# One transformer block on one Trainium2 core: values ahead of transposes in the rounds of neighbourhood attention

## The chip, the cores and the metric

The kernel runs on one core of one Trainium2 chip. A time is device time in microseconds (us) of one execution; the kernel before took 1009.01 us (median of three runs, 1008.9 to 1009.04). Engines are named as the profile names them: PE multiplies matrices (PEld is its weight loads, which overlap its matmuls), DVE and ACT are the vector and scalar engines, POOL is GpSimd, SP issues DMAs.

## The reference

One layer with 1024 latent tokens (16 rows of 64 columns, width 1024) and 256 context tokens. Only the attention matters here; the pooling mixer beside it, the projections and the MLP are the rest of the time.

```python
def row_block(r):                      # one of 16 grid rows; 8 heads of 64
    rs = clip(r - kh // 2, 0, rows - kh)               # a window of 8 rows
    s_loc = einsum('bnqhd,brnkhd->bhnqrk', q_r, k_b) * scale
    s_loc = where(col_mask, s_loc + bias, -inf)        # 16 columns, learned 2-D bias
    s_ctx = einsum('bnqhd,bkhd->bhnqk', q_r, k_ctx) * scale
    p = softmax(concatenate([s_loc, s_ctx], axis=-1))
    o = einsum('bhnqrk,brnkhd->bnqhd', p_loc, v_b) + einsum('bhnqk,bkhd->bnqhd', p_ctx, v_ctx)

mix_x = concatenate([pool_mixer(u_x), attn_x], axis=-1) @ w_out
x = x + gt1 * rmsnorm(mix_x, g_post_mix)
x = x + gt2 * rmsnorm(sq_relu_mlp(modulate(rmsnorm(x))))
```

## The kernel before

The kernel is one program with stages in a row: input norm and projections, attention (212 to 323 us of the span), output projection, MLP. In the attention stage the 16x64 grid is cut into eight tiles of 16 rows by 8 columns (128 tokens). A unit is one pair of heads j (0 to 3) with one tile m (0 to 7); there are N = 32 units, and round i of one loop works on several units at once, at different steps:

- `scores(i)` (L1259, PE): queries times keys for both heads, 12 matmuls of high and low parts, into the two PSUM tiles S (one per head e; there are only these two). An inner tile (m 1 to 6) has 640 keys: three local tiles and the context. An end tile (m 0 and 7) has 512.
- `biased(i, e)` (L1279, DVE): adds the table of biases to S, writes sp to SBUF and its smallest value nm. For e = 0 it also calls `share(i - 1)`: the reciprocal of the sums (L1294, DVE), spread out by POOL as rb (L1296).
- `exps(i, e)` (L1290, ACT): the exponential of sp, in place, with its sums.
- `turn(i)` (L1312, PE): transposes. First rb and, for an inner tile, the fifth key block of each head, into the side columns of pa (256 to 447) and of pz (0 to 191); then four key blocks of both heads into the two PSUM tiles T.
- `fifth_kept(i)` (L1326, ACT): copies the side columns of pa and of pz to px in SBUF.
- `turn_kept(i, 0)` on ACT and `turn_kept(i, 1)` on DVE (L1331): copy the two T tiles to the page pt in SBUF.
- `values(i)` (L1346, PE): the weights pt and px times the values, 8 or 10 matmuls (the profile shows 16 or 20), into columns 0 to 127 of pa, or 128 to 255 for odd i.
- `weighed(i)` (L1356, DVE): those columns of pa times the transposed rb, into the page f.

pa and pz are one PSUM tile of 512 columns each, with one buffer. Each engine runs its instructions in the order in which the code issues them (`in_order` around the loop), and waits between engines are put in by the framework from what instructions read and write. The order of the calls in the loop is therefore the order of the work. Other work of the stage is issued in the rounds, mostly on POOL and SP: bias tables (`built`), key and query parts, sums and loads for later stages. Behind the loop stand the last two units' steps, mixed with the first sums of the output projection (`first_sums`).

Of the kernel before, what the change touches and what calls it, by code (L numbers as in the profile page):

```python
# [108 lines left out]
def hybrid_block(ctx, tc, x, ctx_in, w_mod, mod_pages, w_u, b_mod, gp1, gp2, w_in, pool_w, rpb, w_out, w1, w2, vectors,  # L109
                 mask, edge, out):  # L110
    nc = tc.nc
# [1118 lines left out]
    with (  # L1230
# [12 lines left out]
        def scores(i):  # L1243
            j, m = units[i]
            inner = 0 < m < NM - 1
            n = NKEY if inner else 4 * P
            o = 1 if m == 0 else 0
            q = qparts[j, m // 4]
            ck = [a[:, j * CTX : (j + 1) * CTX] for a in kcs]
            cols = slice((m % 4) * P, (m % 4 + 1) * P)  # L1250
            heads = [slice(e * HD, (e + 1) * HD) for e in range(2)]
            S = [ps_s.tile([P, 1024], F32, tag="S", name=f"S{j}_{m}_{e}") for e in range(2)]
            ts = slice((m - 1) * P, (m + 2) * P) if inner else slice((m + o - 1) * P, (m + o + 1) * P)
            local = [a[:, ts] for a in kparts[j]]
            parts = ((128, local), (512, ck)) if inner else ((0, ck), (256, local))
            for c0, k in parts:
                for n_q, n_k in ((0, 0), (0, 1), (1, 0)):
                    for e, hs in enumerate(heads):
                        nc.tensor.matmul(S[e][:, c0 : c0 + k[0].shape[1]], q[n_q][hs, cols], k[n_k][hs],  # L1259
                                         start=(n_q + n_k == 0), stop=(n_q == 1))  # L1260
            scored[i] = S

        def biased(i, e):
            j, m = units[i]
            inner = 0 < m < NM - 1
            n, o, S = NKEY if inner else 4 * P, 1 if m == 0 else 0, scored[i]
            halves = lambda a: a.rearrange("p (a b) -> p a b", a=2)
            t = tabs[j % 2][e]
            sp = att.tile([P, NKEY], F32, tag="sp", name=f"sp{j}_{m}_{e}", bufs=6)[:, :n]
            if inner:  # L1270
                s, bt, to = S[e][:, 128:768], t[:, :NKEY], sp
            else:
                s, to = halves(S[e][:, 0:512]), halves(sp)
                if o:
                    bt = halves(t[:, 2 * P : 8 * P])[:, :, P:]
                else:
                    bt = halves(t[:, NLOC : NLOC + 512])
            nm = sm(f"nm_{i}_{e}", 1, 6)
            nc.vector.tensor_tensor_reduce(out=to, in0=s, in1=bt, scale=1.0, scalar=BIG, op0=add, op1=ALU.min,  # L1279
                                           accum_out=nm)  # L1280
            probs[i, e] = sp
            least[i, e] = nm
            if e == 0 and i > 0:
                share(i - 1)

        def exps(i, e):
            if e == 0:
                sums[i] = sm(f"su_{i}", 2, 4)
            sp = probs[i, e]
            nc.scalar.activation(sp, sp, AF.Exp, bias=least[i, e], scale=-1.0, accum_out=sums[i][:, e : e + 1])  # L1290
# [11 lines left out]
        def turn(i, t=None, more=None):  # L1302
            inner = 0 < units[i][1] < NM - 1
            if t is None:
                t = [bank(f"T{i}_{h}") for h in range(2)]
            sides = both_sides[i] = more or both_sides[None]
            turned[i] = t
            halves = [slice(h * HD, (h + 1) * HD) for h in range(2)]

            def both(to, src):  # L1310
                for h, hs in enumerate(halves):
                    nc.tensor.transpose(to(h), src(hs), ident[hs, hs])  # L1312

            both(lambda h: sides[h][:, :HD], lambda hs: shares[i][hs])
            for e in range(2 if inner else 0):
                both(lambda h: sides[h][:, (e + 1) * HD : (e + 2) * HD], lambda hs: probs[i, e][hs, 4 * P : 5 * P])
            for c in range(4):
                for e in range(2):
                    o = (4 * e + c) * HD
                    both(lambda h: t[h][:, o : o + HD], lambda hs: probs[i, e][hs, c * P : (c + 1) * P])  # L1320

        def fifth_kept(i):
            n = (3 if 0 < units[i][1] < NM - 1 else 1) * HD
            fifths[i] = att.tile([P, 384], F32, tag="px", name=f"px{i}", bufs=4).rearrange("p (h t) -> p h t", h=2)
            for h in range(2):
                nc.scalar.copy(fifths[i][:, h, :n], both_sides[i][h][:, :n])  # L1326

        def turn_kept(i, h, copy):
            if h == 0:
                turns[i] = page(f"pt{i}").rearrange("p (e i t) -> p e i t", e=2, i=4)  # L1330
            copy(turns[i].rearrange("p e i t -> p (e i) t")[:, :, h * HD : (h + 1) * HD],  # L1331
                 turned[i][h].rearrange("p (a t) -> p a t", a=8))
# [18 lines left out]
        def weighed(i):  # L1351
            j, m = units[i]
            if m == 0:
                heads[j] = page(f"f{j}")
            to = heads[j].rearrange("p (m h t) -> p m h t", h=2, t=HD)[:, m, ::-1, ::-1]
            nc.vector.tensor_tensor(to, pa[:, (i % 2) * P : (i % 2 + 1) * P].rearrange("p (h t) -> p h t", h=2),  # L1356
                                    fifths[i][:, :, :HD], mul)

        N = len(units)
# [88 lines left out]
        with in_order(ET.PE, ET.Activation, ET.DVE, ET.SP) as projected:  # L1448
# [34 lines left out]
            for i in range(N):  # L1483
                if i in LOADS:
                    weight_load(0, kks[LOADS.index(i)])
                if i == N - 2:
                    G1 = gate_page("a")
                if i > 3:
                    weighed(i - 4)
                if i == 0:  # L1490
                    gain = mod_gain(gp1, att.tile([P, 256], F32, tag="gp", name="gpa"), nc.sync)
                    accs["sh"] = page("accsh2")
                    nc.sync.dma_start(accs["sh"], kept_row)
                if i == 2:
                    mod_gate("a", accs["a"], gain, rest_of_bank)
                if i in (5, 6):
                    for k in (2 * i - 10, 2 * i - 9):
                        nc.sync.dma_start(sa2[k], s3[k])
                low()
                scores(i)  # L1500
                biased(i, 0)
                if i < N - 1:
                    biased(i, 1)
                if 8 < i and i % 8 == 3:
                    right_added(i // 8 - 1)
                if 8 < i and i % 8 == 7:
                    add_to(heads[i // 8 - 1][:, :512], sa2[i // 8 - 1])
                for f, *args in jobs.get(i, ()):
                    f(*args)
                if block_copies and (i < 4 or 6 < i):  # L1510
                    block_copied()
                for _ in range(SUMS.count(i)):
                    block_summed()
                if i == 2:
                    late_query = part_page("qP0_1", False)
                    qparts[0, 1] = late_query[:, :512], late_query[:, 512:]
                    high_part(qT[0][1], qparts[0, 1][0])
                if i > 1:
                    turn(i - 2)
                    fifth_kept(i - 2)  # L1520
                if i == 2:
                    turn_kept(0, 0, nc.scalar.copy)
                    column_sums("sc", accs["sc"], lambda name: pa[:, :256])
                if i == N - 1:
                    turn_kept(i - 2, 0, nc.scalar.copy)
                    turn_kept(i - 2, 1, nc.vector.tensor_copy)
                    biased(i, 1)
                exps(i, 0)
                if i == 2:
                    column_sums("sh", accs["sh"], rest_of_bank)  # L1530
                if 2 < i < N - 1:
                    turn_kept(i - 2, 0, nc.scalar.copy)
                exps(i, 1)
                if i == 0:
                    key_parts(2, 0, True, "lo")
                    key_parts(2, 1, True, "lo")
                    query_parts(2, 0, False, "lo")
                if 1 < i < N - 1:
                    turn_kept(i - 2, 1, nc.vector.tensor_copy)
                if i == 2:  # L1540
                    low_part(qT[0][1], *qparts[0, 1])
                for filler in fillers.get(i, ()):
                    last_query(*filler)
                if i > 2:
                    values(i - 3)
            values(N - 3)

            x, s1 = [], halves_of("so1_")

# [989 lines left out]
```

## Time and profile before

| | us |
|---|---|
| median of the runs | 1009.01 |
| profiled execution | 1009.41 |
| its span, first to last instruction | 1007.6 |
| attention: first scores to the start of the last values | 212.6 to 322.4 |
| PE busy / DVE / ACT / POOL, whole span | 997.7 / 799.9 / 580.9 / 208.8 |
| mean granted clock of PE | 0.999 |

A line of the timeline gives the start in us from the span's start, the time in us, the engine, the source line, the operation, output<-inputs, and in brackets the idle time of that engine ahead of it with what ended it. Matmul ends are modelled, so PE reads as nearly always busy; its weight loads (PEld) show when its queue moved. A line of the chain gives start, time, engine, output and source line.

### The profile page before, as it was taken

To read this page: it belongs to the slowest core of one execution; us is meant where nothing else is said; L and a number is where in the kernel's file an instruction comes from. 1 tells how busy PE (TensorE), PEld (TensorE's weight loads), DVE (VectorE), ACT (ScalarE), POOL (GpSimd) and SP (SyncE) were. 2 spreads that over 40 slices of the span, in tenths; PEclk is the share of its full clock that TensorE was granted. 3 is DMA by queue.
4 is the path that set the end of the run, shared out by engine and by line. 5 is a ranking of instruction groups with operands and counts; after the bars stand their busy time and mean duration, and the time that the engine had idled before them with its cause. 6 is when DMAs were issued, how large, how long until landed. Compare 5 with 4: busy or idle time off the path is not lost.

```text
span 1007.6 us, 16671 instructions
## 1 busy us (share of the span) xinstructions
PE 997.7 (99%) x6054; PEld 829.5 (82%) x6054; DVE 799.9 (79%) x1275; ACT 580.9 (58%) x1038; POOL 208.8 (21%) x280
## 2 busy tenths in 40 slices
PE   8999999999999999999999999999999999999997
PEld 5788888879998888888888888888888888888886
DVE  5589766968885689879998888754798888888895
ACT  6673254448886746786555544544656555545551
POOL 4111110167985232410000000101001000022121
PEclk9999999999999999999999999999999999999999
DMA  9999798665999979986776666724999999579944
GB/s 362 394 284 338 238 275 311 211 158 195 225 189 249 233 195 277 294 209 205 261 253 215 201 212 227 230 93 175 317 369 303 308 340 325 170 219 313 319 166 162
DMA packets 146977, 252.49 MB, mean 251 GB/s; under 512 B 10450, under 2 KB 76882, under 8 KB 146896
## 3 DMA queue, kind: packets, MB, share of 16 engines
q1 hardware_dynamic: 111024, 181.63, 52.7%
q0 software_dynamic: 18736, 38.85, 20.1%
q10 hardware_dynamic: 17136, 30.97, 8.3%
q8 instruction: 47, 0.77, 0.3%
q14 instruction: 34, 0.28, 0.1%
HBM read 197.39 MB, written 69.22 MB: 265 GB/s over the span
## 4 chain that ended last, share of the span: by engine, by line
PE 96%; DVE 1%; DMA 1%; ACT 1%; POOL 0%; issue 0%; SPq 0%; DVEq 0%; POOLq 0%; ACTq 0%
PE pu L485 5%; PE pyiM L2400 4%; PE pyiN L2400 4%; PE pa L1346 4%; PE S L1259 3%; PE phx L230 3%; PE phz L230 3%; PE phv L230 3%; PE pyx L231 3%; PE phz L231 3%; PE phv L231 3%; PE phx L232 3%; PE pyx L230 3%; PE pyx L232 3%; PE phx L231 3%; PE phz L232 3%
## 5 line engine op out<-in xcount | busy, mean ns | idle before, releaser
L1966 ACT ACTIVATE c<-c 128x512 f32<-128x512 f32 x48 | 30.3, 631 | 45.3 <-DVE c L2088 26.6
L174 ACT CAST wpS<-S 128x512 fp32r<-128x512 f32 x64 | 38.7, 617 | 28.7 <-PE phv L232 10.1
L1290 ACT ACTIVATE sp<-sp,nm 128x640 f32<-128x640 f32 (+1 forms) x64 | 51.4, 803 | 6.1 <-DVE ri L1294 5.0
L1279 DVE CUSTOM_DVE_ANT_0 sp<-S,tab 128x640 f32<-128x640 f32 (+1 forms) x56 | 44.5, 795 | 13.0 <-PE pz L1312 10.8
L230 PE MATMUL phx<-thB,wpA 128*128 128x512 f32 x128 | 50.2, 392 | 0.0
L180 DVE TENSOR_TENSOR wpS<-S,wpS 128x512 fp32r<-128x512 f32 x64 | 43.4, 686 | 8.2 <-ACT wpS L174 8.2
L232 PE MATMUL phx<-thB,wpA 128*128 128x512 f32 x128 | 49.8, 389 | 0.0
L231 PE MATMUL phx<-tlB,wpA 128*128 128x512 f32 x128 | 49.8, 389 | 0.0
L216 POOL DMA_DIRECT2D t<-in_w x16 | 19.3, 1207 | 131.4 <-DVE b_0l L180 59.1
L1967 ACT ACTIVATE c<-c 128x512 f32<-128x512 f32 x48 | 30.3, 630 | 15.1 <-DVE sa L2051 12.1
L247 POOL MEMSET accb<- 128x1024 f32 x1 | 1.0, 959 | 142.1 <-ACT c L1967 142.1
L230 PEld LDWEIGHTS phx<-thB,wpA 128*128 128x128 f32 x128 | 24.0, 188 | 5.5 <-ACT s L2019 0.4
L232 PEld LDWEIGHTS phx<-thB,wpA 128*128 128x128 f32 x128 | 24.0, 188 | 5.0
L231 PEld LDWEIGHTS phx<-tlB,wpA 128*128 128x128 f32 x128 | 24.0, 188 | 4.9
L1346 PE MATMUL pa<-pt,v 128*64 128x128 f32 x352 | 25.8, 279 | 0.0
L230 PE MATMUL phz<-thB,wpS 128*128 128x512 f32 x64 | 25.0, 391 | 0.0
L230 PE MATMUL phv<-thT,wpA 128*128 128x512 f32 x64 | 25.0, 391 | 0.0
L231 PE MATMUL phz<-tlB,wpS 128*128 128x512 f32 x64 | 24.9, 390 | 0.0
L231 PE MATMUL phv<-tlT,wpA 128*128 128x512 f32 x64 | 24.9, 389 | 0.0
L232 PE MATMUL phz<-thB,wpS 128*128 128x512 f32 x64 | 24.9, 389 | 0.0
L230 PE MATMUL phy<-thT,wpS 128*128 128x512 f32 x64 | 24.9, 389 | 0.0
L231 PE MATMUL phy<-tlT,wpS 128*128 128x512 f32 x64 | 24.9, 389 | 0.0
(1190 smaller groups left out, 3578.1 us busy)
## 6 DMA issues: line engine op xcount, KB each, us to landing
hrA<-hdA SPq DMA_DIRECT2D x24, 512.0 KB, 7.4
wm<-in_mod_pages SPq DMA_DIRECT2D x16, 512.0 KB, 9.3
wa_0w<-in_w SPq DMA_DIRECT2D x16, 512.0 KB, 4.8
wa_1w<-in_w SPq DMA_DIRECT2D x16, 512.0 KB, 4.3
hdA<-c ACTq DMA_DIRECT2D x32, 256.0 KB, 2.2
hdS<-sa ACTq DMA_DIRECT2D x32, 256.0 KB, 2.6
hqS<-sb ACTq DMA_DIRECT2D x32, 256.0 KB, 3.7
b<-in_w SPq DMA_DIRECT2D x16, 512.0 KB, 8.9
```

Of the source, the lines that this page charges most:

```text
L174: nc.scalar.copy(hi, src)
L180: nc.vector.tensor_tensor(lo, src, hi.bitcast(F32), sub)
L230: nc.tensor.matmul(ps, ahi, bhi, start=first, stop=False, skip_group_check=more)
L231: nc.tensor.matmul(ps, ahi, blo, start=False, stop=False, skip_group_check=more)
L232: nc.tensor.matmul(ps, alo, bhi, start=False, stop=last, skip_group_check=more)
L485: nc.tensor.matmul(pus[b][j], wk(wgt, k, low, j * P, P), r, start=(k == 0 and n == 0), stop=(k == KT - 1 and n == 2))
L1279: nc.vector.tensor_tensor_reduce(out=to, in0=s, in1=bt, scale=1.0, scalar=BIG, op0=add, op1=ALU.min, accum_out=nm)
L1290: nc.scalar.activation(sp, sp, AF.Exp, bias=least[i, e], scale=-1.0, accum_out=sums[i][:, e : e + 1])
L1346: nc.tensor.matmul(pa[e * HD : (e + 1) * HD, cols], v[:, f : f + HD], turns[i][:, e, c] if c < 4 else fifths[i][:, :, (e + 1) * HD : (e + ...
L1966: nc.scalar.activation(r, src, AF.Relu)
L1967: nc.scalar.activation(r, r, AF.Square)
L2400: nc.tensor.matmul(to, a[part][:, j * 256 + t * P : j * 256 + (t + 1) * P], r, start=h + j == 0 and n < 2, stop=ends and n > 1)
```

## The change

In the rounds from 5 on, the products with the values of unit i - 4 are issued right behind the scores of unit i, and the transposes of unit i - 2 behind them; before, the transposes came behind the scores, and then the values of unit i - 3. The weighing of unit i - 4, which stood at the head of a round, is issued behind both biased scores. The side copies of unit i - 2 move behind both exponentials, and so does ACT's copy of T. Rounds 0 to 3 are as before; round 4 has no values; and two units' values are left to be issued behind the loop, in place of one.

```diff
-                if i > 3:
-                    weighed(i - 4)
+                if i == 4:
+                    weighed(0)
...
                 scores(i)
+                if i > 4:
+                    values(i - 4)
                 biased(i, 0)
                 if i < N - 1:
                     biased(i, 1)
+                if i > 4:
+                    weighed(i - 4)
...
                 if i > 1:
                     turn(i - 2)
+                if 1 < i < 4 or i == N - 1:
                     fifth_kept(i - 2)
...
                 exps(i, 0)
...
-                if 2 < i < N - 1:
+                if i == 3:
                     turn_kept(i - 2, 0, nc.scalar.copy)
                 exps(i, 1)
+                if 3 < i < N - 1:
+                    fifth_kept(i - 2)
+                    turn_kept(i - 2, 0, nc.scalar.copy)
...
-                if i > 2:
-                    values(i - 3)
-            values(N - 3)
+                if i == 3:
+                    values(0)
+            for i in (N - 4, N - 3):
+                values(i)
```

In the built programs, names are those of the steps above (v and vc are values of latent and context tokens, kP and kc the keys, qP the queries), and the brackets name the engines whose semaphores an instruction waits for. PE in round 6, before: from the last scores to the first transposes.

```order
L1259 MATMUL S_6_0_2548<-kP0h,qP_1_2282 128x384 [waits DVE_49]
L1259 MATMUL S_6_1_2549<-kP0h,qP_1_2282 128x384 [waits DVE_49]
...
L1259 MATMUL S_6_0_2548<-kch,qP_1_2282 128x256
L1259 MATMUL S_6_1_2549<-kch,qP_1_2282 128x256
L1312 MATMUL pa<-ident,rb_2487 128x64 [waits DVE_49,Pool_49]
L1312 MATMUL pz<-ident,rb_2487 128x64 [waits Activation_49]
L1312 MATMUL pa<-ident,sp_4_0_2409 128x64
```

And now, at the same place:

```order
L1259 MATMUL S_6_0_2537<-kP0h,qP_1_2282 128x384 [waits PE_49]
L1259 MATMUL S_6_1_2538<-kP0h,qP_1_2282 128x384 [waits PE_49]
...
L1259 MATMUL S_6_0_2537<-kch,qP_1_2282 128x256
L1259 MATMUL S_6_1_2538<-kch,qP_1_2282 128x256
L1346 MATMUL pa<-pt_2452,v_1179 64x128 [waits Activation_49]
L1346 MATMUL pa<-pt_2452,v_1179 64x128
L1346 MATMUL pa<-pt_2452,v_1180 64x128 x4
L1346 MATMUL pa<-pt_2452,vc 64x128 x2
L1346 MATMUL pa<-px_2449,vc 64x128 x2
L1312 MATMUL pa<-ident,rb_2486 128x64 [waits DVE_49,Pool_49]
L1312 MATMUL pz<-ident,rb_2486 128x64 [waits Activation_49]
```

The ten matmuls of values have moved between scores and transposes, and the scores wait for no DVE semaphore any more. DVE in the same round, before (ISA is the biased score and the reading of its smallest value):

```order
L1356 TENSOR_TENSOR f_2393<-pa,px_2446 128x128 [waits PE_49,Activation_49]
L1279 ISA sp_6_0_2562,nm_0_2563<-S_6_0_2548,tab_1993 128x640 [waits DVE_49,PE_49]
L1279 ISA nm_0_2563 128x1
L1294 RECIPROCAL ri_2565<-su_2529 128x2 [waits Activation_49,Pool_49]
L1279 ISA sp_6_1_2569,nm_1_2570<-S_6_1_2549,tab_1994 128x640 [waits DVE_49,PE_49]
L1279 ISA nm_1_2570 128x1
L1331 COPY pt_2606<-T_1_2578 128x8x64 [waits DVE_49,PE_49]
```

And now:

```order
L1279 ISA sp_6_0_2561,nm_0_2562<-S_6_0_2537,tab_1993 128x640 [waits DVE_49,PE_49]
L1279 ISA nm_0_2562 128x1
L1294 RECIPROCAL ri_2564<-su_2526 128x2 [waits Activation_49,Pool_49]
L1279 ISA sp_6_1_2568,nm_1_2569<-S_6_1_2538,tab_1994 128x640 [waits DVE_49,PE_49]
L1279 ISA nm_1_2569 128x1
L1356 TENSOR_TENSOR f_2393<-pa,px_2449 128x128 [waits PE_49,Activation_49]
L1331 COPY pt_2607<-T_1_2578 128x8x64 [waits DVE_49,PE_49]
```

The weighing f stands behind both biased scores, ahead of the copy of T. ACT in the same round, before:

```order
L1326 COPY px_2601<-pa 128x192 [waits DVE_49,PE_49]
L1326 COPY px_2601<-pz 128x192 [waits PE_49]
L1290 ACTIVATE sp_6_0_2562,su_2604<-sp_6_0_2562,nm_0_2563 128x640 [waits DVE_49,Activation_49]
L1331 COPY pt_2606<-T_0_2577 128x8x64 [waits PE_49,Activation_49]
L1290 ACTIVATE sp_6_1_2569,su_2604<-sp_6_1_2569,nm_1_2570 128x640 [waits DVE_49,Activation_49]
```

And now:

```order
L1290 ACTIVATE sp_6_0_2561,su_2601<-sp_6_0_2561,nm_0_2562 128x640 [waits DVE_49,Activation_49]
L1290 ACTIVATE sp_6_1_2568,su_2601<-sp_6_1_2568,nm_1_2569 128x640 [waits DVE_49,Activation_49]
L1326 COPY px_2604<-pa 128x192 [waits DVE_49,PE_49]
L1326 COPY px_2604<-pz 128x192 [waits PE_49]
L1331 COPY pt_2607<-T_0_2577 128x8x64 [waits PE_49]
```

The side copies, which waited for the transposes ahead of the first exponential, now follow the second.

## The prediction

> **What bounds the kernel now.** I read the page first (busy times, the chain that ended last), then the chain in order of time inside the attention stage, then the timeline of single rounds there, engine by engine.
>
> ```profile
> PE 997.7 (99%) x6054; PEld 829.5 (82%) x6054; DVE 799.9 (79%) x1275; ACT 580.9 (58%) x1038; POOL 208.8 (21%) x280
> PE 96%; DVE 1%; DMA 1%; ACT 1%; POOL 0%; issue 0%; SPq 0%; DVEq 0%; POOLq 0%; ACTq 0%
> ...
> 276.72 1.09 PE S L1259 x12
> 277.99 0.50 PE T L1312 x16
> 278.49 1.24 PE pa L1346 x20
> 279.73 1.08 PE S L1259 x12
> ```
>
> TensorE is the bound. In the chain a round of attention (here round 22) is scores, transposes, values, scores, with no other engine between: 3.01 us a round, all of it PE. One inner round closely, first PE's weight loads, which show when the queue really moves, then DVE:
>
> ```profile
> 276.64 0.18 PEld L1259 LDWEIGHTS S<-kP2h,qP 64*128 64x128 f32 x2 [0.17 <-DVE nm L1279]
> 277.40 0.19 PEld L1259 LDWEIGHTS S<-kch,qP 64*128 64x128 f32 x2
> 277.54 0.14 PEld L1312 LDWEIGHTS pa<-ident,rb 64*128 64x128 f32 x1
> 277.77 0.58 PEld L1312 LDWEIGHTS T<-ident,sp 64*128 64x128 f32 x16
> 278.42 0.64 PEld L1346 LDWEIGHTS pa<-pt,v 128*64 128x64 f32 x12
> 279.66 0.19 PEld L1259 LDWEIGHTS S<-kP2h,qP 64*128 64x128 f32 x2 [0.17 <-DVE nm L1279]
> ...
> 277.10 0.28 DVE L1356 TENSOR_TENSOR f<-pa,px 128x128 f32<-128x128 f32 x1
> 277.84 0.82 DVE L1279 CUSTOM_DVE_ANT_0 sp<-S,tab 128x640 f32<-128x640 f32 x1 [0.47 <-PE pz L1312]
> 278.67 0.80 DVE L1279 CUSTOM_DVE_ANT_0 sp<-S,tab 128x640 f32<-128x640 f32 x1
> 279.40 0.08 DVE L1279 DVE_READ_ACCUMULATOR2_ANT nm<- 128x1 f32 x1
> 279.40 0.69 DVE L1331 COPY pt<-T 128x512 f32<-128x512 f32 x1
> ```
>
> So PE spends 0.90 us on scores (276.64 to 277.54), 0.88 on the transposes, 1.24 on the values. DVE's two biased scores run beside the transposes and values: the first starts 1.20 after the scores' first load (277.84), the second is through at 2.76 (279.40). The weighing f (L1356) is done at 277.38, 0.16 before the transposes load. Everything DVE does has cover, and the next scores find their banks free just in time.
>
> **The change: what it makes late.** Values move ahead of the transposes, and on DVE the weighing moves behind both biased scores. The transposes write the tile pa (columns 256 on), the weighing reads pa (columns 0 to 255). Is one held up by the other? The trace shows a guard on the whole of pa, at the first values of the loop:
>
> ```profile
> 228.34 0.31 ACT L1326 COPY px<-pa 128x192 f32<-128x192 f32 x1
> 228.54 0.34 ACT L1326 COPY px<-pz 128x192 f32<-128x192 f32 x1
> 228.71 0.42 PEld L1346 LDWEIGHTS pa<-pt,vc 128*64 128x64 f32 x8 [0.27 <-ACT px L1326]
> ```
>
> These values write columns 0 to 127 and read older copies; the copy that ended at 228.65 read columns 256 on, and they still waited 0.27 for it, not for the pz copy, which ran to 228.88. So a write to any column of pa waits for a reader of any other, and the first transpose waits for the weighing. The orders agree: the first transpose names a DVE semaphore in both programs, and in the new one the scores no longer need one, because the transposes ahead of them have already waited past both biased scores. A round then becomes a closed loop with no cover: scores, biased, biased, weighing, transposes, next scores.
>
> The Trainium skill ("PSUM — Partial Sum Buffer", the rule behind its bank collisions) asks for semaphores on PSUM by bank and 32-partition quadrant, not by address: by it the time is that of this loop, and with a guard by address that of the first rival. The 0.27 us above agrees.
>
> Price of an inner round from one load of scores to the next:
> - to the end of the second biased score 2.76 (above). DVE starts its next instruction in that same hundredth (279.40, twice);
> - the weighing 0.28: to 3.04;
> - DVE to PE 0.06. No row has exactly this wait; two near ones have:
>
> ```profile
> 250.26 0.40 PEld L1259 LDWEIGHTS S<-kP1h,qP 64*128 64x128 f32 x2 [0.17 <-issue]
> 250.34 0.08 DVE L1279 DVE_READ_ACCUMULATOR2_ANT nm<- 128x1 f32 x1
> 239.47 0.30 POOL L1296 COPY rb<-ri 128x128 f32<-128x128 f32 x1
> 239.82 0.14 PEld L1312 LDWEIGHTS pa<-ident,rb 64*128 64x128 f32 x1 [0.31 <-POOL rb L1296]
> ```
>
>  The pair of score loads at 250.26 ends at 250.66, so its second began at 250.48, 0.06 after the row that ended at 250.42; and 239.77 to 239.82 is 0.05. Taken 0.06: to 3.10;
> - the transposes, from first load to the next scores' load: 277.54 to 277.77, then 16 loads in 0.58 of which the last 0.14 overlaps what follows, then one step of 0.03: 0.70.
>
> Sum 3.80, against 3.01. The values (0.90 to 2.14 in the round) now lie wholly beside DVE; PE stands still for about 0.9 us a round. The end rounds of a head pair have smaller tiles:
>
> ```profile
> 238.74 0.19 PEld L1259 LDWEIGHTS S<-kch,qP 64*128 64x128 f32 x2 [0.17 <-DVE nm L1279]
> 239.75 0.69 DVE L1279 CUSTOM_DVE_ANT_0 sp<-S,tab 128x512 f32<-128x512 f32 x1 [0.39 <-PE S L1259]
> 241.04 0.08 DVE L1279 DVE_READ_ACCUMULATOR2_ANT nm<- 128x1 f32 x1
> ...
> 245.61 0.14 PEld L1312 LDWEIGHTS pa<-ident,rb 64*128 64x128 f32 x1
> 245.71 0.58 PEld L1312 LDWEIGHTS T<-ident,sp 64*128 64x128 f32 x16
> ```
>
> Small scores: 2.30 to the end of biasing, plus 0.28, 0.06 and 0.70: 3.34. Small transposes: 0.57 in place of 0.70: 3.67. Rounds 5 to 30 hold six with small scores (7, 8, 15, 16, 23, 24), six with small transposes (9, 10, 17, 18, 25, 26) and 14 full ones: 6 x 3.34 + 6 x 3.67 + 14 x 3.80 = 95.3 us. Before, these 26 rounds ran from the scores of round 5 to those of round 31:
>
> ```profile
> 229.73 0.19 PEld L1259 LDWEIGHTS S<-kP0h,qP 64*128 64x128 f32 x2 [0.17 <-DVE nm L1279]
> 232.74 0.18 PEld L1259 LDWEIGHTS S<-kP0h,qP 64*128 64x128 f32 x2 [0.17 <-DVE nm L1279]
> 308.91 0.19 PEld L1259 LDWEIGHTS S<-kch,qP 64*128 64x128 f32 x2 [0.17 <-DVE nm L1279]
> ```
>
> 308.91 - 232.74 = 76.2. Loss: 19.1 us.
>
> **The edges.** Round 4 loses its values: PE has 0.90 + 0.70, so the biased scores bind (2.76 + 0.08 + 0.06 = 2.90, was 3.01): -0.1. Those values come back behind the loop, where PE is busy throughout: +1.24. In round 31 only the first biased score stands ahead of the weighing (1.01 + 0.69 from the small scores' rows, 0.28, 0.06: 2.04), while scores and values fill PE to about the same time: nothing. Sum 19.1 - 0.1 + 1.24 = +20.2 us.
>
> **What costs nothing.** ACT's side copies (L1326) move behind both exponentials:
>
> ```profile
> 278.77 0.83 ACT L1290 ACTIVATE sp<-sp,nm 128x640 f32<-128x640 f32 x1 [0.21 <-DVE ri L1294]
> 279.60 0.56 ACT L1331 COPY pt<-T 128x512 f32<-128x512 f32 x1
> 281.03 0.32 ACT L1326 COPY px<-pa 128x192 f32<-128x192 f32 x1
> 281.24 0.33 ACT L1326 COPY px<-pz 128x192 f32<-128x192 f32 x1
> ```
>
> ACT starts at 2.13 of the round (278.77), runs two exponentials to 3.79, side copies to 4.44 and its T copy to 5.0, which is 1.2 of the next round, whose transposes need the banks at 3.10. If that 1.9 us of cover were gone, the copies would join the loop. DVE's T copy starts when the transposes are through (about 4.0) and takes 0.69, to 4.7, ahead of the next biased score at 3.80 + 1.20 = 5.0. The share copies on POOL, waited for 0.31 us in round 7, get 1.2 us more. No DMA is moved by the edit. The pages of transposed weights live a little longer and some are handed on differently; the loads behind them get 20 us more, and PE has no long wait for any load afterwards, so nothing is gained there either.
>
> **Rivals.**
> - The wait isn't there, or is hidden (guard by columns). Then PE stays the bound, with values +1.24 behind the loop, about -0.1 in round 4, and the POOL wait gone: about 1009.8. Against it stands 228.71. Chance 0.06.
> - Faster: PE's pauses ahead of the scores are true waits for DVE, and the new order hides them with no new wait.
>
> ```profile
> PEld S L1259 <- DVE nm L1279: 2.6, 15, 0.2
> PEld S L1259 <- issue: 1.4, 8, 0.2
> ```
>
>  That would save up to 4.0 us of rounds 8 to 31, less 1.2: about 1006. Against it: the eight put down to "issue", with DVE long done, are as long (0.17), so it is a cost of turning from values to scores. It decides only if the first transpose doesn't wait. Chance 0.03.
> - Slower still: PE, idle a quarter of each round, gets a lower clock. At half clock scores and transposes take 0.90 and 0.70 more, 26 x 1.6 = 42: about 1071.
>
> ```profile
> 7.50:10.00 2.50, 1.47 (x11) 1.06 (x11) 1.68 (x4) 2.28 (x5) 1.99 (x2) 1.00 1.02 419
> 1000.00:1007.60 7.60, 1.67 (x14) 1.47 (x13) 2.04 (x5) 0.77 (x3) 0.00 (x0) 0.93 0.34 125
> ```
>
>  With PE busy 1.47 of 2.50 us the granted clock stayed 1.00; only the last 7.6 us, with 1.67 busy, show 0.93. Pauses of 0.9 us should leave it. The Trainium skill ("TensorE: Matmul & The Clock Gate", the second failure mode) tells of a kernel whose frequent short pauses for PSUM made the gate swing, which would be this rival. Chance 0.04.
> - A longer loop (the ACT or DVE copies of T join it): 0.4 us more a round, about 1040. Chance 0.04.
>
> **The numbers.** The forecast has the remaining 0.83. The profiled execution took 1009.41 around a span of 1007.6, 0.4 above the median of the runs, 1009.01; the +20.2 is added to the median: 1029.2 us. Its bounds: turning from transposes to scores may cost a switch like that from values to scores (0.17 idle; 26 x 0.17 = 4.4) and the handover 0.05 more (1.3): 1035. The other way, 0.2 us a round of loads drawn ahead or DVE overlap (5.2): 1024. Range 1023 to 1036, which leaves out the rivals and some of the forecast's own tail, 2 in 10. About 0.2% (2 us) is what a measurement tells from no change: faster 0.03 (the second rival), same 0.05 and slower 0.92, the first rival's last 0.01 being slower.
>
> **What will show it.** In the changed kernel's trace the first transposes' loads (L1312, pa<-ident,rb) should have idle time ahead of them in rounds 5 to 30, near 0.9 us each and some 22 in total, put down to DVE f (L1356); scores should start every 3.8 us, f 2.76 us behind the first load of scores; the loads of scores should have no idle ahead of them; PE's clock should stay 1.00, and PE past the attention stage should run as before, 20 us later. The prediction is wrong if the transposes follow the values at once, if the clock row falls, or if ACT is what the transposes wait for.

## The result and the profile after

The changed kernel took 1031.76 us (median of 4 runs, 1031.39 to 1032.48) against 1009.01 before: 1.0226 times the time before, 95% interval 1.0209 to 1.0244, some 22.7 us more. The forecast was 1029.2, range 1023 to 1036. The profiled execution took 1031.39 around a span of 1029.6, which is 22.0 above the span before.

The page of the changed kernel: the busy time of each engine, the shares of the chain that ended last, and the granted clock in 40 slices (9 is 90% or more).

```profile
PE 998.8 (97%) x6054; PEld 828.0 (80%) x6054; DVE 802.6 (78%) x1275; ACT 579.3 (56%) x1038; POOL 208.5 (20%) x280
...
PEclk9999999999999999999999999999999999999999
...
PE 91%; issue 3%; DVE 2%; DMA 2%; POOL 1%; ACT 1%; SPq 0%; DVEq 0%; POOLq 0%; ACTq 0%
```

No engine has more instructions than before, PE is busy 1.1 us more and DVE 2.7 us more, the clock is the same, and the span is 22 us longer. PE's share of the chain fell from 96% to 91%; issue took three points of it, and DVE, DMA and POOL about one each. One inner round (round 20; the prediction prices the same round, from 276.64 on, and calls it 22), PE's weight loads first, then DVE, then ACT:

```profile
287.56 0.22 PEld L1259 LDWEIGHTS S<-kP2h,qP 64*128 64x128 f32 x2
...
289.06 0.47 PEld L1346 LDWEIGHTS pa<-pt,v 128*64 128x64 f32 x8
290.71 0.14 PEld L1312 LDWEIGHTS pa<-ident,rb 64*128 64x128 f32 x1 [1.18 <-POOL rb L1296]
...
291.39 0.22 PEld L1259 LDWEIGHTS S<-kP2h,qP 64*128 64x128 f32 x2
...
288.75 0.82 DVE L1279 CUSTOM_DVE_ANT_0 sp<-S,tab 128x640 f32<-128x640 f32 x1 [0.20 <-PE S L1259]
290.31 0.08 DVE L1279 DVE_READ_ACCUMULATOR2_ANT nm<- 128x1 f32 x1
290.31 0.28 DVE L1356 TENSOR_TENSOR f<-pa,px 128x128 f32<-128x128 f32 x1
291.68 0.69 DVE L1331 COPY pt<-T 128x512 f32<-128x512 f32 x1 [1.09 <-PE T L1312]
...
289.68 0.83 ACT L1290 ACTIVATE sp<-sp,nm 128x640 f32<-128x640 f32 x1 [1.19 <-DVE ri L1294]
291.73 0.59 ACT L1331 COPY pt<-T 128x512 f32<-128x512 f32 x1
```

This is the predicted loop. The round is 3.83 us (287.56 to 291.39): 2.75 to the end of biasing (290.31), 0.28 for f, 0.12 from its end (290.59) to the first transpose's load (290.71), 0.68 for the transposes to the next scores, which have no idle ahead of them. The values' last loads end at 289.53, wholly inside DVE's stretch, and PE stands still for 1.18 behind them. ACT is through in time, and waits itself.

The groups of the first transposes, PE and then PEld: busy and mean ns, then the idle time ahead and what ended most of it.

```profile
L1312 PE MATMUL pa<-ident,rb 64*128 64x64 f32 x32 | 7.8, 243 | 20.1 <-DVE f L1356 12.2
...
L1312 PEld LDWEIGHTS pa<-ident,rb 64*128 64x128 f32 x32 | 4.3, 136 | 26.2 <-POOL rb L1296 15.6
```

The loads idle 26.2 us in all, 25.1 of it in rounds 5 to 30, 0.77 to 1.19 in each; 0.9 each and some 22 in total were predicted. The two rows name two releasers, f on DVE for the matmul and rb on POOL for its load. Which one holds it can't be read from a name, since the instruction waits for both; in the round above f ends 0.12 ahead of the load, and the runs below take f out of the way, or make it longer.

### The profile page after: what moved, and what is told of

It is laid out like the page before. It is cut to its first block, busy times and chain, and to the rows that moved or that the text cites. A ratio compares the mean times of both kernels' runs of the same rounds, so it can differ in the third digit from the quotient of the medians.

```text
span 1029.6 us, 16667 instructions
## 1 busy us (share of the span) xinstructions
PE 998.8 (97%) x6054; PEld 828.0 (80%) x6054; DVE 802.6 (78%) x1275; ACT 579.3 (56%) x1038; POOL 208.5 (20%) x280
## 4 chain that ended last, share of the span: by engine, by line
PE 91%; issue 3%; DVE 2%; DMA 2%; POOL 1%; ACT 1%; SPq 0%; DVEq 0%; POOLq 0%; ACTq 0%
PE pu L485 4%; PE pyiM L2409 4%; PE pyiN L2409 4%; PE phx L230 3%; PE phz L230 3%; PE phv L230 3%; PE pyx L231 3%; PE phx L232 3%; PE pyx L230 3%; PE pyx L232 3%; PE phv L231 3%; PE phz L231 3%; PE phx L231 3%; PE phz L232 3%; PE phv L232 3%; PE S L1259 3%
## 5 line engine op out<-in xcount | busy, mean ns | idle before, releaser
L1331 DVE COPY pt<-T 128x512 f32<-128x512 f32 x31 | 21.4, 691 | 30.5 <-PE T L1312 29.4
L1312 PE MATMUL pa<-ident,rb 64*128 64x64 f32 x32 | 7.8, 243 | 20.1 <-DVE f L1356 12.2
L1312 PEld LDWEIGHTS pa<-ident,rb 64*128 64x128 f32 x32 | 4.3, 136 | 26.2 <-POOL rb L1296 15.6
L230 PE MATMUL phv<-thT,wpA 128*128 128x512 f32 x64 | 25.0, 391 | 0.0
L232 PE MATMUL phv<-thT,wpA 128*128 128x512 f32 x64 | 24.9, 389 | 0.0
```

What stands on the lines that cost most here:

```text
L230: nc.tensor.matmul(ps, ahi, bhi, start=first, stop=False, skip_group_check=more)
L232: nc.tensor.matmul(ps, alo, bhi, start=False, stop=last, skip_group_check=more)
```

## The experiments

Five kernels test the loop; two more follow up what the last of these, the weighing alone moved, brought up. The kernel before took 1009.6 to 1009.8 us beside them.

**The weighing issued behind the transposes.** The order on PE, DVE and ACT stays that of the changed kernel; but since the weighing is now written later in the code than the transposes, it waits for them and no longer they for it. (`right_added`, which reads f, moves with it, and a load on POOL then comes ahead of its DMAs in three rounds.)

```diff
-                if i > 4:
-                    weighed(i - 4)
                 if 8 < i and i % 8 == 3:
...
                 if i > 1:
                     turn(i - 2)
+                if i > 4:
+                    weighed(i - 4)
```

> The changed kernel with one call moved: the weighing of unit i - 4 is issued behind the transposes of unit i - 2 instead of ahead of them. The order on every engine stays what it is in the changed kernel; only the direction of one wait turns round (the weighing now waits for the side transposes, and no transpose for the weighing). Theory (the transposes wait for the weighing because both touch the tile pa): PE is the bound again, a full round 3.01 us, no idle ahead of the transposes' loads, and the time 1009.2 us, 1008.5 to 1010.5 (1009.0 with 1.24 of values more behind the loop, less the POOL wait of 0.3 and 0.1 to 0.2 in three rounds that DVE bound). Rival (the transposes wait for something else that the new order made late, such as the biased scores, POOL's rb or ACT's copies): the time stays near 1031.8.

Measured: 1012.18 us (6 runs), 1.0030 times before (1.0018 to 1.0043). So some 20 of the 22.7 us were this one wait. PE in round 21, then the weighing on DVE:

```profile
280.06 0.19 PEld L1259 LDWEIGHTS S<-kP2h,qP 64*128 64x128 f32 x2
281.17 0.64 PEld L1346 LDWEIGHTS pa<-pt,v 128*64 128x64 f32 x12 [0.15 <-ACT px L1326]
282.41 0.14 PEld L1312 LDWEIGHTS pa<-ident,rb 64*128 64x128 f32 x1 [0.17 <-issue]
283.09 0.19 PEld L1259 LDWEIGHTS S<-kP2h,qP 64*128 64x128 f32 x2
...
282.92 0.29 DVE L1356 TENSOR_TENSOR f<-pa,px 128x128 f32<-128x128 f32 x1
```

The transposes follow the values with only the 0.17 that stood ahead of the scores before the change, f starts 0.51 after their first load, and the round is 3.03, against 3.01. Yet the time lies 2.5 above before, and above the range given. Most of that is at the end of the loop, shown here in this kernel; the last line is the kernel before:

```profile
309.58 0.19 PEld L1259 LDWEIGHTS S<-kch,qP 64*128 64x128 f32 x2
310.68 0.64 PEld L1346 LDWEIGHTS pa<-pt,v 128*64 128x64 f32 x12 [0.32 <-ACT px L1326]
313.13 0.64 PEld L1346 LDWEIGHTS pa<-pt,v 128*64 128x64 f32 x12 [0.43 <-ACT px L1326]
315.46 0.19 PEld L230 LDWEIGHTS pox<-wo_0h,mix 128*128 128x128 f32 x1 [0.17 <-issue]
...
312.84 0.19 PEld L230 LDWEIGHTS pox<-wo_0h,mix 128*128 128x128 f32 x1 [0.17 <-issue]
```

From the last round's scores to the first sums of the projection it takes 5.88 us, against 3.93 before (308.91 to 312.84): 1.24 are the second unit's values, and 0.75 are two waits of values for the side copies of pa, which read other columns of it. It is the same guard, with the values as the writer that waits and the copies on ACT as the readers. Some 0.7 more is lost in the rounds (79.84 from the scores of round 4 to those of round 31, against 79.18), where values wait for those copies too, 2.9 in all, while the pauses ahead of the scores are mostly gone.

**The sixteen T transposes ahead of the side ones.** `turn` writes T first and pa and pz last; all else is the changed kernel.

```diff
-            both(lambda h: sides[h][:, :HD], ...)
-            for e in range(2 if inner else 0):
-                both(lambda h: sides[h][:, (e + 1) * HD : (e + 2) * HD], ...)
             for c in range(4):
                 ...
+            both(lambda h: sides[h][:, :HD], ...)
+            for e in range(2 if inner else 0):
+                both(lambda h: sides[h][:, (e + 1) * HD : (e + 2) * HD], ...)
```

> The changed kernel with the transposes of a unit in another order: the 16 that write the two T tiles first, the 2 to 6 that write the side columns of pa and pz last. Theory (only writes to pa wait for the weighing): the T transposes run right behind the values while DVE still works, and the round is 2.75 + 0.28 + 0.12 and then only the side loads, 0.20 in a full round: 3.35 in place of 3.83, with small scores 3.0, in all -12.3 us: 1019.5, between 1017 and 1022. Rival (all transposes wait, for DVE's biased scores or its copies of T): no change, 1031.8.

Measured: 1020.38 us (one run), inside the range given. The loads of T and of the side transposes, the next scores, and f:

```profile
284.07 0.58 PEld L1312 LDWEIGHTS T<-ident,sp 64*128 64x128 f32 x16 [0.17 <-DVE ri L1294]
285.08 0.14 PEld L1312 LDWEIGHTS pa<-ident,rb 64*128 64x128 f32 x1 [0.44 <-issue]
285.27 0.22 PEld L1259 LDWEIGHTS S<-kP2h,qP 64*128 64x128 f32 x2
...
284.68 0.28 DVE L1356 TENSOR_TENSOR f<-pa,px 128x128 f32<-128x128 f32 x1
```

The transposes into T don't wait for f: their loads start 0.61 ahead of it. The first one into pa does, and its load starts 0.12 after f ends (284.96 to 285.08). So the wait belongs to the tile pa, not to the step. The rule that the prediction cited from the Trainium skill ("PSUM — Partial Sum Buffer", bank collisions) is to guard by bank and quadrant, not by address. This run agrees with it: the transposes write columns 256 on, f reads columns below 256, and still the transposes wait. Whether the guard goes by the tile or by a bank, no run here tells.

**ACT's order as before.** Side copies, exponential, copy of T, exponential, in the changed kernel.

```diff
-                if 1 < i < 4 or i == N - 1:
+                if i > 1:
                     fifth_kept(i - 2)
...
-                if i == 3:
+                if 2 < i < N - 1:
                     turn_kept(i - 2, 0, nc.scalar.copy)
                 exps(i, 1)
-                if 3 < i < N - 1:
-                    fifth_kept(i - 2)
-                    turn_kept(i - 2, 0, nc.scalar.copy)
```

> The changed kernel with ACT's order put back: side copies, exponential, copy of T, exponential. Theory (ACT then joins the loop: side copies wait for the late transposes, both exponentials stand behind them, and DVE's reciprocal, which stands between the two biased scores of the next round, waits for the second exponential): from the transposes' load 0.45 to the side copies, 0.42 for them, 0.83 and 0.47 for exponential and copy, 0.92 for the second exponential, 0.14 to the second biased score, 0.73 for it, 0.28 and 0.12 to the next transposes: 4.36 us a round in place of 3.83, in all +14 us: 1046, between 1040 and 1050. Rival (ACT's order is off the path, as idle time of 1.2 us a round suggests): 1031.8, within 1 us.

Measured: 1046.55 us (one run). The side copies and the share's reciprocal, which DVE runs between the two biased scores:

```profile
283.58 0.32 ACT L1326 COPY px<-pa 128x192 f32<-128x192 f32 x1 [1.73 <-PE pz L1312]
...
286.05 0.17 DVE L1294 RECIPROCAL ri<-su 128x2 f32<-128x2 f32 x1 [0.19 <-ACT sp L1290]
```

ACT's exponentials now stand behind side copies that wait for the late transposes, and DVE waits for their sums: ACT is in the loop. So moving the copies behind the exponentials kept the changed kernel from losing 15 us more.

**The weighing twice.** One more `weighed(i - 4)` behind the one in the changed kernel.

> The changed kernel with every weighing from round 5 on issued twice, back to back on DVE, with the same result into the same place. Theory (the weighing stands in the loop that sets the round): a second one behind the first adds about 0.21 us (two of them took 0.49 in a row of before, one 0.28), in 27 rounds 5.7: 1037.5 (1036 to 1039.5). Rival (DVE has cover in the changed kernel, and the rounds are set elsewhere): 1031.8.

Measured: 1040.55 us (4 runs), 1.0304 times before (1.0289 to 1.0320), 8.8 above the changed kernel and 1 above the range given. The pair took, in two rounds:

```profile
291.73 0.61 DVE L1356 TENSOR_TENSOR f<-pa,px 128x128 f32<-128x128 f32 x2
...
295.88 0.48 DVE L1356 TENSOR_TENSOR f<-pa,px 128x128 f32<-128x128 f32 x2
```

What the second one adds, 0.33 or 0.20, goes into the round in full, as the loop has it: rounds are 4.16 or 4.03, in place of 3.83. The forecast had only the 0.20. So it is f that the transposes wait for: when f grows, the round grows by as much, although POOL's rb is the same. Why the pair takes longer in some rounds was not followed.

**The weighing alone moved.** The kernel before, with the weighing behind both biased scores and nothing else; transposes stay ahead of values. First one run, then four.

```diff
-                if i > 3:
-                    weighed(i - 4)
                 if i == 0:
...
                 if i < N - 1:
                     biased(i, 1)
+                if i > 3:
+                    weighed(i - 4)
```

> The kernel before with one call moved: the weighing of unit i - 4 is issued behind both biased scores, as in the change; values stay behind the transposes and ACT's order stays. Theory (the place of the weighing on DVE makes the wait): the transposes wait for it in every round from 4 on, and the values, now behind them, have no cover either: 2.75 + 0.28 + 0.12 + 0.88 + 1.24 = 5.27 us for a full round in place of 3.01, 4.8 for one with small scores, in all +59 us: 1068, between 1062 and 1073. Rival (the move of the values makes the wait): near 1009.

> The same kernel as the run with the weighing alone moved, timed more often, to see how far its 1104 is a property of the kernel. Theory (the pauses lower the clock in every execution): 1095 to 1115, granted clock of the attention rounds under 0.85. Rival (a disturbance of that one execution): 1068, clock 1.00.

Measured: 1104.45 us, and again 1106.73 (1103.87 to 1108.60), 1.0967 times before (1.0948 to 1.0985). The place of the weighing alone makes the wait, without any move of the values. But the times lie 36 to 39 us above the 1068 that the loop explains. From the second profile, a window of the rounds (its length; busy us of PE, PEld, DVE, ACT, POOL with counts; granted clock; DMA share; GB/s), and PE there:

```profile
240.00:400.00 160.00, 110.97 (x1308) 96.38 (x1306) 61.68 (x175) 63.68 (x177) 65.84 (x104) 0.77 0.45 96
...
278.86 0.29 PEld L1259 LDWEIGHTS S<-kP1h,qP 64*128 64x128 f32 x2 [0.33 <-issue]
...
282.46 0.14 PEld L1312 LDWEIGHTS pa<-ident,rb 64*128 64x128 f32 x1 [2.20 <-POOL rb L1296]
282.64 0.61 PEld L1312 LDWEIGHTS T<-ident,sp 64*128 64x128 f32 x16
283.32 1.15 PEld L1346 LDWEIGHTS pa<-pt,v 128*64 128x64 f32 x12
285.65 0.29 PEld L1259 LDWEIGHTS S<-kP1h,qP 64*128 64x128 f32 x2 [0.33 <-issue]
```

The pause ahead of the transposes is 2.20 here, since no values fill it, and behind it the values' loads take 1.15 where 0.64 was usual, about half the rate. The granted clock is 0.77 on average, and this round takes 6.8 us (278.86 to 285.65) in place of 5.27.

**The pause filled, and the same work outside it.** Two kernels from the last one. In the first the values of unit i - 4 are computed a second time between scores and transposes, inside the pause; in the second, values(i - 3) are computed twice in a row, outside it.

```diff
                 scores(i)
+                if i > 4:
+                    values(i - 4)          # first kernel
                 biased(i, 0)
...
                 if i > 2:
                     values(i - 3)
+                if i > 4:
+                    values(i - 3)          # second kernel
```

> The kernel before with the weighing alone moved behind both biased scores (the run that took 1104, 36 us over its forecast of 1068, at a granted clock near 0.74 in the attention rounds), and from round 5 on the values of unit i - 4 are computed a second time, with the same result into the same columns of pa, in the pause of PE between the scores and the transposes. That is 27 x 1.24 = 33 us more of PE work. Theory (the 36 us are the clock, and the clock fell because PE paused about 2.2 us in each round): the second values take 1.24 of that pause, the loop over DVE stays 5.27 us long, the clock stays at 1.00, and the time falls to 1068 (1062 to 1074), with more work done. Rival one (the 36 us are another wait, not the clock): 1104 or more. Rival two (the clock falls because TensorE waits at all in a closed loop, whatever the length of the pause): clock under 0.9, over 1090.

> The kernel before with the weighing alone moved behind both biased scores, and from round 5 on every unit's values computed twice in a row, right behind each other: the same extra PE work as in the run with the filled pause, but outside the pause of 2.2 us, which stays as it was. The extra 1.24 us stands in the loop, so at full clock 1070 + 27 x 1.24 = 1103. Theory (the clock falls by the length of the pause together with the transposes, which ends about 3 us after the last scores): the clock of the attention rounds stays under 0.9, and about 3.4 us of each round pass at half rate, 1.6 us lost in each: 1140 (1125 to 1155). Rival (the clock goes by the share of a round in which PE is busy, here about 0.55 as in the changed kernel): clock 1.00, 1103 (1097 to 1109).

Measured: 1070.88 us with the pause filled (4 runs; 1.0602 times before, 1.0586 to 1.0618), and 1118.03 with the work outside it (2 runs; 1.1072, 1.1040 to 1.1104). Windows and PE's loads, first of the one, then of the other:

```profile
232.00:236.00 4.00, 3.02 (x44) 2.66 (x46) 1.52 (x4) 2.62 (x7) 1.51 (x4) 0.78 0.32 120
240.00:360.00 120.00, 102.24 (x1704) 88.34 (x1699) 58.38 (x166) 61.08 (x168) 62.62 (x100) 1.00 0.58 120
...
295.04 0.14 PEld L1312 LDWEIGHTS pa<-ident,rb 64*128 64x128 f32 x1 [0.82 <-POOL rb L1296]
295.90 0.63 PEld L1346 LDWEIGHTS pa<-pt,v 128*64 128x64 f32 x12
```

```profile
240.00:400.00 160.00, 114.98 (x1647) 104.84 (x1649) 56.66 (x161) 58.77 (x163) 62.51 (x101) 0.86 0.43 88
...
297.10 0.14 PEld L1312 LDWEIGHTS pa<-ident,rb 64*128 64x128 f32 x1 [2.20 <-POOL rb L1296]
297.96 0.64 PEld L1346 LDWEIGHTS pa<-pt,v 128*64 128x64 f32 x12
303.43 0.18 PEld L1312 LDWEIGHTS pa<-ident,rb 64*128 64x128 f32 x1 [2.20 <-POOL qP L1126]
304.83 1.15 PEld L1346 LDWEIGHTS pa<-pt,v 128*64 128x64 f32 x12
```

With the pause cut to 0.7 to 1.2 us (0.82 in the round shown) the clock is back at 1.00 and the kernel is 36 us faster, while PE does some 30 us more work: the excess was the clock. Round 4 of this kernel, which has no second values yet, still has a pause of 2.20, and the clock from 232 to 236 is 0.78. With the same work outside, the pause stays 2.20 and the clock falls to 0.86, so the length of the pause is what counts, not the work. Nor is it the share of a round that PE stands still: 1.83 of 4.49 us (0.41), in the run with ACT's old order, left the clock at 1.00, and 2.20 of 6.33 (0.35) here did not. But both expectations for this last kernel missed (1140 and 1103): 13 of the rounds 5 to 30 take 5.8 to 6.4 us, and 13 take 7.2 to 9.6. The same pause is followed by half the rate in one round and not in the next; what decides it the traces don't show.

## Why the prediction was right, point by point

- **The loop and its cause**: right. The wait of the first transposes for the weighing, through the shared tile, is worth some 20 of the 22.7 us (first run), the transposes into T don't have it (second run), and a longer weighing makes it longer (the weighing twice).
- **The inner round**, 3.80 predicted, 3.83 measured. The step that was off is the handover from DVE to PE, 0.06 there and 0.12 here. It was taken from waits for other producers (a reading of the minimum, a POOL copy); behind f it is 0.12 in the run with the T transposes first too. The range had allowed for 0.05 more here, and for 0.17 ahead of the scores, which didn't come.
- **The small scores' rounds**, 3.34 predicted, are 3.47. There biasing is through at 2.32, and f still waits for the values, which the prediction overlooked:

```profile
239.65 0.23 PEld L1259 LDWEIGHTS S<-kch,qP 64*128 64x128 f32 x2
241.42 0.25 PEld L1346 LDWEIGHTS pa<-px,vc 128*64 128x64 f32 x4
242.44 0.14 PEld L1312 LDWEIGHTS pa<-ident,rb 64*128 64x128 f32 x1 [0.77 <-POOL rb L1296]
...
241.97 0.08 DVE L1279 DVE_READ_ACCUMULATOR2_ANT nm<- 128x1 f32 x1
242.03 0.29 DVE L1356 TENSOR_TENSOR f<-pa,px 128x128 f32<-128x128 f32 x1
```

 f starts 2.38 after the scores' first load, not at 2.30, and behind it the handover is 0.12 again, not 0.06. f starts 0.61 after the values' last group of loads does (241.42), the same as in round 31 below (330.52 to 331.13), where the trace names the values as what f waits for.
- **Rounds 4 to 30 together**: predicted +19.0 (19.1 less 0.1). Measured, from the scores of round 4 to those of round 31, 99.54 against 79.18 (229.73 to 308.91): +20.4. Here two errors cancel in part: round 4 takes 2.07 and not 2.90, since the scores of round 5 already start at 231.28, and round 5 takes 4.55 and not 3.80, since its transposes stand where the loop puts them all the same. Together the two take 6.62, and 6.70 was predicted; that these two rounds come out so near is luck.

```profile
229.21 0.19 PEld L1259 LDWEIGHTS S<-kP0h,qP 64*128 64x128 f32 x2 [0.17 <-DVE nm L1279]
328.75 0.23 PEld L1259 LDWEIGHTS S<-kch,qP 64*128 64x128 f32 x2
330.52 0.25 PEld L1346 LDWEIGHTS pa<-px,vc 128*64 128x64 f32 x4
331.54 0.14 PEld L1312 LDWEIGHTS pa<-ident,rb 64*128 64x128 f32 x1 [0.77 <-POOL rb L1296]
334.73 0.19 PEld L230 LDWEIGHTS pox<-wo_0h,mix 128*128 128x128 f32 x1 [0.17 <-issue]
...
331.13 0.29 DVE L1356 TENSOR_TENSOR f<-pa,px 128x128 f32<-128x128 f32 x1 [0.58 <-PE pa L1346]
```

- **The end of the loop**: predicted +1.24, measured 5.98 (328.75 to 334.73) against 3.93, +2.05. The values behind the loop were sized rightly; "round 31 nothing" was the error. There too f waits for values to leave PE (0.58), and the transposes for f (0.77).
- **The sum**: +20.4, +2.05, 0.1 past the first sums (694.9 to the end of the span against 694.8), less 0.5 by which this execution reached round 4 earlier, is the 22.0 of the span. The stage behind the loop is as before.
- **The first rival** (a guard by columns, so no wait: 1009.8) didn't come. The first run, which takes the wait away by the order of the code, is the nearest to it, at 1012.2. It doesn't test the rival's price: its waits of values for side copies come from the guard on the whole tile, which the rival has not.
- **The faster rival** (1006) didn't come. It was to decide only if the transposes don't wait. In the first run they don't, and the 0.17 stands ahead of the transposes (282.41) in place of the scores, so it goes with the turn from values to what follows, as the prediction argued.
- **The ACT rival** (1040) didn't come: in the round shown ACT's last copy ends at 292.32, and the next transposes load over 2 us later (290.71 and one round of 3.83). With ACT's old order ACT does join the loop (1046.5).
- **The clock rival** (1071) didn't come either, at pauses of 1.2 us; pauses of 2.2 us did lower the clock, in kernels other than this one. Its price, with every round at half clock, was not tested.

## What to carry to other kernels

When work on a shared buffer is moved behind a long chain of another engine, ask who writes any part of that buffer next; an engine that was merely hidden becomes a link of a loop, and every 0.1 us in it counts once a round. The cheap cure is the order in the code: with the reader written behind the writer, the same instructions in the same order on PE, DVE and ACT lost 2.5 us in place of 22.7. And a pause of TensorE can have a second price beside its length, as those of 2.2 us had here, so work that fills it can be free or better.

## What was not expected of the hardware

Pauses of PE of about 1.2 us in a round of 3.8, and up to 1.8 in the 4.4 us rounds of the run with ACT's old order, left the clock at 1.00; pauses of 2.2 us let it fall to 0.77 on average (0.86 with the second values outside the pause). In that kernel half rate also follows a pause of 1.93, in a round with small scores (the values' loads at 263.14 take 1.15), while no pause up to 1.83 was followed by it in the run with ACT's old order. The clock can fall right at the end of such a pause: at 303.43, behind 2.20 us, the first transpose's load takes 0.18, not 0.14, and the values' loads behind it take 1.15. The Trainium skill ("TensorE: Matmul & The Clock Gate", Why this matters for your kernels) warns of idle gaps above about 3 us; here 2.20 was enough, in half the rounds of one kernel and in nearly all of the other. Its Part 4 (PE-mode transpose) says that transposes do not count as PE-busy in the same way. If that held for these, the gap would be 3.06 (from the end of the last scores' load, 280.26, to the values, 283.32). In the round at 282.46, where T's loads still run at full rate (0.61) and the values' do not, the two readings can't be told apart; in the round at 303.43 the clock fell as the transposes began, so there the 2.20 were enough without them.
